# A hybrid mLSTM and sparse-attention block on one core: the first head's products placed later, and the relative-bias rows from split products over the full array

## The chip, the core and the metric
The kernel runs on one core of one Trainium2 chip. The core has a matrix engine (TensorE; PE in the profile, with its weight loads listed as PEld), a vector engine (DVE), a scalar engine (ACT), GpSimd (POOL), a synchronisation engine (SP) that here only issues DMAs, and 16 DMA engines. Every engine works through its own list of instructions in order; an instruction that waits for a semaphore holds up everything behind it on that engine. The metric is the device time of one execution in microseconds.

## The reference, cut to what matters
The block normalises x, multiplies it by one wide input matrix and splits the result into a chunked mLSTM branch (4 heads) and a sparse-attention branch (8 heads); both are gated, mixed and projected, and a gated feed-forward layer follows. Two pieces matter here. In the mLSTM, each head of 1024 positions is cut into 8 chunks of 128:

```python
log_d = jnp.where(causal, bc[..., :, None] - bc[..., None, :] + ic[..., None, :], -jnp.inf)
m_i = jnp.maximum(jnp.max(log_d, axis=-1), log_inter)
P = jnp.exp(log_d - m_i[..., None]) * jnp.einsum('bhcid,bhcjd->bhcij', qc, kc)
num = (jnp.einsum('bhcij,bhcjv->bhciv', P, vc)
       + s_inter[..., None] * jnp.einsum('bhcid,bhcdv->bhciv', qc, C_prev))
```

In the attention, a table of 32 buckets by 8 heads gives a bias for each distance between query and key, the same along every diagonal:

```python
table = rel_bias.astype(jnp.float32).T.reshape(G, R, REL_BUCKETS)
lw = einsum(qb, k_wb) + table[:, :, rel_bucket(dist)]
```

## The kernel before, in words
Stage A normalises and transposes x into two parts whose sum is x (UTH and UTL, in the format that TensorE reads in one pass) and makes the mLSTM values. Stage B, where the change lies, does two things side by side. `b_dense` makes 16 tiles of 128 output columns (q, k and o of each head, and four for the attention). Each tile is two halves of 512 positions; a half is 8 steps, and a step is three products (L277 to L279), called dense products below. `b_aux` makes the gates, then the four mLSTM heads one after the other (`core`), and between them, one at a time from a list called `spare`, the rows of the relative bias (`rel_rows`).

The order is fixed when the program is built. `driver` writes the instructions of both streams into one list: each number that `b_aux` yields is an amount of dense work to be written before it goes on (a dense step counts 648). So a yield moves everything after it, on every engine.

For each dense tile, ScalarE rounds the raw weights into `whi` (L248) and GpSimd makes the rest `wlo` in four instructions (L254): this is the weight split of the tile that comes next. When a half of a q or k tile is done, ScalarE moves it out of PSUM (`padq`, `padk`, L523) and VectorE runs the four-tap convolution on it, one L528 and three L530. Once k is complete, ScalarE loads another function table, applies silu to q and k (L532, L533) and loads the first table again.

A head of the mLSTM: two tables of 128x1024, MB and SB, come from DRAM through SP. GpSimd turns MB into the mask (L682), causal minus MB. `st_a(c)` makes the chunk's product `pa` on TensorE, `E` on ScalarE from the mask (L695), and `PT` and `KW` on VectorE (L698, L699). `st_b(c)` multiplies them with the values into `pn` (L704) and updates the state `CN`; ScalarE copies `pn` to `nd` and squares it (`jk`). A yield of 5000 stands ahead of the first head's `st_a(0)`.

`rel_rows` has four rounds of 480 columns. SP loads a one-hot piece `OH` of 33 rows (L652), TensorE multiplies it with `relt`, 33 rows by 8 heads in plain float32 (L654), VectorE copies the 8 rows out (`rrow`, L656) and GpSimd stores them (`d_row`, L657). Afterwards GpSimd spreads each head's row over 128 rows of DRAM (`d_rep`, L660), which the attention reads much later.

The later stages (gates, attention, output projection and feed-forward by fast matrix multiplication) are not touched by the change.

Of the kernel before, what the change touches and what calls it, by code (L numbers as in the profile page):

```python
# [8 lines left out]
F32 = mybir.dt.float32  # L9
F32R = mybir.dt.float32r  # L10
AF = mybir.ActivationFunctionType
ALU = mybir.AluOpType
PSUM = bass.MemoryType.PSUM

P = 128
T = 1024
NT = 8
# [4 lines left out]
NH = 8  # L22
# [20 lines left out]
def cast32(ap):  # L43
    return ap.bitcast(F32)
# [114 lines left out]
def body(ctx, tc, a, out, stop=None, dbg=None):  # L159
    nc = tc.nc  # L160
# [12 lines left out]
    causal = cst[:, 1, :]  # L173
# [98 lines left out]
    def split_evict(hi, lo, src):  # L272
        nc.scalar.activation(hi, src, AF.Copy)
        nc.vector.tensor_tensor(lo, src, cast32(hi), ALU.subtract)
# [74 lines left out]
    with ExitStack() as sa:  # L349
# [139 lines left out]
        bp = pb_.enter_context(tc.tile_pool(name="stB", bufs=1, reuse_waits="tile"))  # L489
# [75 lines left out]
            for nm, j in order_b1:  # L565
                yield from b_tile(nm, j)

        relt = bp.tile([33, NH], F32, name="relt")
        nc.vector.memset(relt, 1.0)
        nc.scalar.dma_start(relt[0:32, :], a["rel_bias"])  # L570

        def gates():

# [72 lines left out]

        def rel_rows():

            for s in range(4):
                sl = slice(480 * s, 480 * s + 480)  # L650
                OH = bp.tile([33, 480], F32, name=f"OH{s}", tag="OH", bufs=2)
                nc.sync.dma_start(OH, a["oh"][:, sl])  # L652
                pb = psB.tile([P, 512], F32, name=f"pb{s}", tag="Y", bufs=1)
                nc.tensor.matmul(pb[0:NH, 0:480], relt, OH, start=True, stop=True)  # L654
                rrow = bp.tile([NH, 480], F32, name=f"rrow{s}", tag="rrow", bufs=2)
                nc.vector.tensor_copy(rrow, pb[0:NH, 0:480])  # L656
                nc.gpsimd.dma_start(d_row[:, sl], rrow)  # L657
                yield 2600.0
            for h in range(NH):
                nc.gpsimd.dma_start(d_rep[h], d_row[h, :].partition_broadcast(P))  # L660
                yield 650.0

        MBS = {}
        spare = []

        def core_load(h):
            MB = bp.tile([P, NT, P], F32, name=f"MB{h}", tag="MB", bufs=2)
            SB = bp.tile([P, NT, P], F32, name=f"SB{h}", tag="SB", bufs=2)
            for d_, s_ in ((d_M, MB), (d_S, SB)):
                r0 = d_[h:h + 1, :]  # L670
                nc.sync.dma_start(s_, bass.AP(tensor=r0.tensor, offset=r0.offset, ap=[[0, P], [4 * P, NT], [1, P]]))
            MBS[h] = MB, SB

        def core(h, other):

            MB, SB = MBS[h]
# [2 lines left out]
            q3 = qT[h].rearrange("p (c t) -> p c t", c=NT)  # L679
            k3 = kT[h].rearrange("p (c t) -> p c t", c=NT)  # L680
            dec = bp.tile([P, NT], F32, name=f"dec{h}", tag="dec", bufs=2)
            nc.gpsimd.tensor_tensor(MB, causal[:, None, :].to_broadcast([P, NT, P]), MB, ALU.subtract)  # L682
            nc.vector.tensor_copy(dec, SB[:, :, 127])
            nc.vector.tensor_tensor(SB, q3, SB, ALU.mult)
            nd = bp.tile([P, NT, MD + 1], F32, name=f"nd{h}", tag="nd", bufs=2)
# [31 lines left out]
                j_ = bp.tile([P, P], mybir.dt.bfloat16, name=f"jk{h}{c}", tag="jk", bufs=2)  # L717
                nc.scalar.activation(j_, nd[:, c, 0:MD], AF.Square, accum_out=ss[:, 0, c:c + 1])

            yield 5000.0 if h == 0 else 3000.0  # L720
            for c in range(2):
                st_a(c)
                yield 1300.0
# [58 lines left out]
        def b_aux():  # L782
            rel = rel_rows()
            other = []
            spare.extend([lambda: next(rel)] * 12)
            yield from gates()
            core_load(0)
            for h in range(MH):
                if h + 1 < MH:
                    core_load(h + 1)  # L790
                yield from core(h, other)
            while spare:
                spare.pop(0)()
            while other:
                if not other[0][0]():
                    yield None
                else:
                    other.pop(0)[1]()
                    yield 2600.0

        driver(b_dense(), b_aux())
        pb_.close()
        for h in range(4):
# [44 lines left out]
    with ExitStack() as sb:  # L848
        bp = sb.enter_context(tc.tile_pool(name="stB2", bufs=1, reuse_waits="tile"))
# [93 lines left out]
    with ExitStack() as sc:  # L943
# [323 lines left out]
        while any(queues.values()):  # L1267
# [20 lines left out]
            _, op, st = cand  # L1288
# [408 lines left out]
    pb = {}  # L1697
# [242 lines left out]
```

## Time and profile before

| what | value |
|---|---|
| time, median of 3 runs (range) | 1605.21 us (1604.78 to 1607.33) |
| profiled execution: its own time / its span | 1604.37 us / 1602.6 us |
| TensorE busy in the span | 1558.8 us, 97% |
| VectorE / ScalarE / GpSimd busy | 1046.7 (65%) / 742.3 (46%) / 230.7 us (14%) |
| granted TensorE clock, mean | 0.992 of full speed |

The page lists busy time by engine, the span in 40 slices, the chain of work that ended last, and the costliest groups of instructions. Beside it the trace answers questions: who waited for whom, the instructions of an engine in order of time, and the busy times and granted clock in chosen stretches. Stage B lies at about 97 to 320 us of the span; the first head's mask and the four rounds of `rel_rows` lie at 129 to 165 us. Where TensorE is busy nearly all the time, each microsecond in which it waits, or in which its clock is lower, is read in that stretch.

### The profile page before, as it was taken

How to read it: one execution, taken by the hardware profiler on the slowest of the kernel's cores; microseconds unless marked ns; L12 is line 12 of the kernel's file. 1: busy time of each engine (PE TensorE's matmuls, PEld its weight loads, DVE VectorE, ACT ScalarE, POOL GpSimd, SP SyncE). 2: the span in 40 equal slices, each digit the busy share in tenths (PEclk: the TensorE clock that was granted, in tenths of full speed). 3: DMA queues.
4: the chain of work that ended last, by engine and by line, in shares of the span. 5: the costliest groups of instructions: out<-in, count | busy, mean ns of one | idle time of the engine just before them, and what ended most of it. 6: DMA issues, size and time to landing. Idle time of an engine off the chain costs nothing.

```text
span 1602.6 us, 21999 instructions
## 1 busy us (share of the span) xinstructions
PE 1558.8 (97%) x7858; PEld 1317.6 (82%) x7858; DVE 1046.7 (65%) x2214; ACT 742.3 (46%) x1560; POOL 230.7 (14%) x355
## 2 busy tenths in 40 slices
PE   6999999989999999999999989999999999999997
PEld 6876888878989888878887878888888888888876
DVE  6446553235989688840454498666676666978996
ACT  5215455324888688842344244333333333454442
POOL 4013434420113111013000022000000000000130
PEclk9999999999999999999999999999999999999999
DMA  8004532792236422163447212222322223750202
GB/s 254 3 25 100 152 117 97 243 230 86 67 93 103 115 68 85 47 230 106 144 145 269 73 67 92 80 91 80 120 91 79 79 85 113 276 189 22 105 1 105
DMA packets 147358, 181.44 MB, mean 113 GB/s; under 512 B 10414, under 2 KB 105040, under 8 KB 147248
## 3 DMA queue, kind: packets, MB, share of 16 engines
q1 hardware_dynamic: 137440, 157.31, 31.4%
q0 software_dynamic: 9472, 22.06, 5.5%
q8 instruction: 62, 1.02, 0.3%
q10 hardware_dynamic: 336, 0.66, 0.1%
q14 instruction: 48, 0.39, 0.1%
HBM read 137.95 MB, written 49.90 MB: 117 GB/s over the span
## 4 chain that ended last, share of the span: by engine, by line
PE 85%; DVE 3%; DMA 2%; ACT 1%; issue 0%; POOL 0%; SPq 0%; DVEq 0%; ACTq 0%
PE PS L278 15%; PE PS L279 15%; PE PS L277 15%; PE d L277 7%; PE d L279 7%; PE d L278 7%; PE T L1059 4%; PE obank L1081 2%; PE obank L1079 2%; PE br L278 1%; PE br L277 1%; PE br L279 1%; DMA d_ql<-lnq 1%; PE pn L704 1%; DMA raw<-in_w_out 0%; PE pa L692 0%
## 5 line engine op out<-in xcount | busy, mean ns | idle before, releaser
L277 PE MATMUL d<-UTH,whi 128*128 128x512 f32 x576 | 234.4, 407 | 1.8 <-ACT mg L938 0.7
L279 PE MATMUL d<-UTH,wlo 128*128 128x512 f32 x576 | 226.1, 392 | 0.0
L278 PE MATMUL d<-UTL,whi 128*128 128x512 f32 x576 | 225.4, 391 | 0.0
L1441 DVE TENSOR_TENSOR sl<-PS,sl 128x512 f32<-128x512 f32 x182 | 123.8, 687 | 94.9 <-PE PS L279 92.2
L254 POOL TENSOR_TENSOR wlo<-raw,whi 128x256 fp32r<-128x256 f32 x124 | 96.6, 808 | 323.7 <-ACT whi L248 289.9
L279 PEld LDWEIGHTS d<-UTH,wlo 128*128 128x128 f32 x576 | 108.6, 188 | 24.0
L277 PEld LDWEIGHTS d<-UTH,whi 128*128 128x128 f32 x576 | 109.2, 190 | 20.6 <-ACT mg L938 2.0
L278 PEld LDWEIGHTS d<-UTL,whi 128*128 128x128 f32 x576 | 109.3, 190 | 17.2
L1068 DVE TENSOR_TENSOR TL<-T,TH 128x512 fp32r<-128x512 f32 (+1 forms) x184 | 103.3, 581 | 28.8 <-ACT TH L1064 27.9
L1064 ACT ACTIVATE TH<-T 128x512 fp32r<-128x512 f32 (+1 forms) x184 | 90.2, 510 | 26.5 <-PE T L1059 23.6
L1441 DVE TENSOR_TENSOR sl<-sl,sl 128x512 f32<-128x512 f32 (+1 forms) x113 | 77.3, 690 | 17.8 <-ACT sl L1444 12.5
L1444 ACT ACTIVATE sl<-sl 128x512 f32<-128x512 f32 (+1 forms) x85 | 53.4, 631 | 72.0 <-PE PS L278 47.1
L1441 POOL TENSOR_TENSOR acc<-acc 128x512 f32<-128x512 f32 x6 | 9.2, 1546 | 503.5 <-DVE acc L1441 503.4
L1444 ACT ACTIVATE wh<-sl 128x512 fp32r<-128x512 f32 x61 | 38.5, 630 | 81.2 <-PE PS L278 70.0
L1079 PE MATMUL obank<-TH,VHL 128*128 128x256 f32 x264 | 75.6, 310 | 0.0
L1081 PE MATMUL obank<-TL,VHL 128*128 128x256 f32 x264 | 68.4, 283 | 0.4 <-DVE TL L1068 0.4
L277 PE MATMUL PS<-q 128*128 128x512 f32 x172 | 66.9, 389 | 0.0
L278 PE MATMUL PS<-q 128*128 128x512 f32 x172 | 66.9, 389 | 0.0
L279 PE MATMUL PS<-q 128*128 128x512 f32 x172 | 66.9, 389 | 0.0
L1403 DVE TENSOR_TENSOR q<-br,q 128x512 f32<-128x512 f32 x32 | 21.9, 688 | 67.4 <-ACT q L1396 47.4
L1444 ACT ACTIVATE q<-sl 128x512 fp32r<-128x512 f32 x74 | 43.5, 624 | 46.5 <-PE PS L278 29.1
L1441 DVE TENSOR_TENSOR q<-sl,q 128x512 fp32r<-128x512 f32 x72 | 50.2, 734 | 2.8 <-ACT q L1444 2.7
(1289 smaller groups left out, 4256.2 us busy)
## 6 DMA issues: line engine op xcount, KB each, us to landing
raw<-in_w_in SPq DMA_DIRECT2D x40, 512.0 KB, 4.6
ra<-in_w_gate SPq DMA_DIRECT2D x22, 512.0 KB, 5.2
d_gu<-sl SPq DMA_DIRECT2D x44, 256.0 KB, 2.1
q<-d_mg SPq DMA_DIRECT2D x32, 256.0 KB, 3.0
d_rep<-d_row POOLq DMA_DIRECT2D x8, 960.0 KB, 10.3
sl<-d_gu SPq DMA_DIRECT2D x15, 512.0 KB, 5.1
sl<-in_w_down SPq DMA_DIRECT2D x15, 512.0 KB, 5.5
ra<-in_w_up SPq DMA_DIRECT2D x11, 512.0 KB, 3.5
```

Of the source, the lines that this page charges most:

```text
L254: nc.gpsimd.tensor_tensor(lo[:, zs], v[:, zs], cast32(hi)[:, zs], ALU.subtract)
L277: nc.tensor.matmul(ps, ah, bh, start=first, stop=False)
L278: nc.tensor.matmul(ps, ah, bl, start=False, stop=False)
L279: nc.tensor.matmul(ps, al, bh, start=False, stop=last)
L1059: nc.tensor.transpose(pt[:, z, P * r:P * r + P], e, ident)
L1064: nc.scalar.activation(hl[0][:, 0:m], pt[:, 0:m], AF.Copy)
L1068: nc.vector.tensor_tensor(hl[1][:, 0:m], pt[:, 0:m], cast32(hl[0])[:, 0:m], ALU.subtract)
L1079: nc.tensor.matmul(po, vv, th[:, z, :], start=(st[1] == 0), stop=False)
L1081: nc.tensor.matmul(po, vv, tl[:, z, :], start=False, stop=(st[1] == st[2]))
L1403: nc.vector.tensor_tensor(sg[b], ps, sg[b], ALU.mult)
L1441: return pl.step(alts, lambda e: ENG[e].tensor_tensor(out_(), x(), y(), alu), reads, writes, **kw)
L1444: return pl.step((("ACT", cost),), lambda e: nc.scalar.activation(out_(), x(), fn), reads, writes, **kw)
```

## The change
Four edits, all in stage B.

1. The first head's mask is taken out of `core` and called right after the loads of its tables are issued (`mask(0)` in `b_aux`); the other heads call it where it was.
2. The yield ahead of the first head's `st_a(0)` grows from 5000 to 7000.
3. `relt` becomes 128 rows by 128 columns, zero outside the 33 by 8, in two parts (`split_evict`: ScalarE makes the high part, VectorE the low one). It is made when the first round starts, not ahead of the stage.
4. `OH` becomes 128 rows: GpSimd clears it and then issues its load itself (before, SP did). Each round is two products of 128x480 in the one-pass format, and `rrow` has one buffer where it had two.

```diff
-        relt = bp.tile([33, NH], F32, name="relt")
-        nc.vector.memset(relt, 1.0)
-        nc.scalar.dma_start(relt[0:32, :], a["rel_bias"])
+        relr = bp.tile([P, P], F32, name="relr")
+        relt = bp.tile([P, 2, P], F32R, name="relt")
+        nc.vector.memset(relr, 0.0)
+        nc.vector.memset(relr[32:33, 0:NH], 1.0)
+        nc.scalar.dma_start(relr[0:32, 0:NH], a["rel_bias"])
...
         def rel_rows():
+            split_evict(relt[:, 0, :], relt[:, 1, :], relr)
             for s in range(4):
                 sl = slice(480 * s, 480 * s + 480)
-                OH = bp.tile([33, 480], F32, name=f"OH{s}", tag="OH", bufs=2)
-                nc.sync.dma_start(OH, a["oh"][:, sl])
+                OH = bp.tile([P, 480], F32R, name=f"OH{s}", tag="OH", bufs=2)
+                nc.gpsimd.memset(cast32(OH), 0.0)
+                nc.gpsimd.dma_start(OH[0:33, :], a["oh"][:, sl])
                 pb = psB.tile([P, 512], F32, name=f"pb{s}", tag="Y", bufs=1)
-                nc.tensor.matmul(pb[0:NH, 0:480], relt, OH, start=True, stop=True)
-                rrow = bp.tile([NH, 480], F32, name=f"rrow{s}", tag="rrow", bufs=2)
+                for z in range(2):
+                    nc.tensor.matmul(pb[:, 0:480], relt[:, z, :], OH, start=(z == 0), stop=(z == 1))
+                rrow = bp.tile([NH, 480], F32, name=f"rrow{s}", tag="rrow", bufs=1)
                 nc.vector.tensor_copy(rrow, pb[0:NH, 0:480])
                 nc.gpsimd.dma_start(d_row[:, sl], rrow)
...
+        def mask(h):
+            MB, _ = MBS[h]
+            nc.gpsimd.tensor_tensor(MB, causal[:, None, :].to_broadcast([P, NT, P]), MB, ALU.subtract)
...
-            nc.gpsimd.tensor_tensor(MB, causal[:, None, :].to_broadcast([P, NT, P]), MB, ALU.subtract)
+            if h > 0:
+                mask(h)
...
-            yield 5000.0 if h == 0 else 3000.0
+            yield 7000.0 if h == 0 else 3000.0
...
             core_load(0)
+            mask(0)
             for h in range(MH):
```

The yield alone moves instructions on every engine, so the built order is shown at three places. The first is VectorE where the first head begins: qT is the convolution of the second head's q (two halves), PT_0 and KW_0 belong to chunk 0 of the first head. Before:

```order
L530 SCALAR_TENSOR_TENSOR qT_1088<-padq_1086,COLS,qT_1088 128x512 x3
L698 TENSOR_TENSOR PT_0_1175<-pa_0_1170,E_0_1173 128x128
L699 TENSOR_SCALAR KW_0_1176<-pa_0_1170,E_0_1173 128x128
L528 TENSOR_SCALAR qT_1088<-padq_1086,COLS 128x512
L530 SCALAR_TENSOR_TENSOR qT_1088<-padq_1086,COLS,qT_1088 128x512 x3
```

The same place now:

```order
L530 SCALAR_TENSOR_TENSOR qT_1090<-padq_1088,COLS,qT_1090 128x512 x3
L528 TENSOR_SCALAR qT_1090<-padq_1088,COLS 128x512
L530 SCALAR_TENSOR_TENSOR qT_1090<-padq_1088,COLS,qT_1090 128x512 x3
L709 TENSOR_TENSOR PT_0_1197<-pa_0_1192,E_0_1195 128x128
L710 TENSOR_SCALAR KW_0_1198<-pa_0_1192,E_0_1195 128x128
```

The second half's convolution has moved from behind PT_0 and KW_0 to ahead of them. On TensorE, nine dense products have moved from behind the first `pn` to ahead of the first `pa`.

The second place is GpSimd from the first head's mask (MB) to the end of the bias rounds; what an instruction waits for stands in brackets (a name is a semaphore: an engine's, or a DMA's). Before:

```order
L254 TENSOR_TENSOR wlo_1116<-raw_998,whi_1115 128x256 x3
L682 TENSOR_TENSOR MB_1125<-cst,MB_1125 128x1024 [waits DMAHW5_49]
...
L254 TENSOR_TENSOR wlo_1236<-raw_1093,whi_1235 128x256 [waits PE_49,DMAHW3_49,Activation_49,Pool_49]
L657 DMA d_row<-rrow_1260 8x480 [waits DMASW6_49,DVE_49]
...
L657 DMA d_row<-rrow_1384 8x480 [waits DMASW1_49,DVE_49]
L254 TENSOR_TENSOR wlo_1409<-raw_1197,whi_1408 128x256 [waits PE_49,DMAHW1_49,Activation_49,Pool_49]
```

The same place now:

```order
L254 TENSOR_TENSOR wlo_1118<-raw_1000,whi_1117 128x256 x3
L682 TENSOR_TENSOR MB_1127<-cst,MB_1127 128x1024 [waits DMAHW5_49]
...
L254 TENSOR_TENSOR wlo_1223<-raw_1095,whi_1222 128x256 [waits PE_49,DMAHW3_49,Activation_49,Pool_49]
L656 MEMSET OH_1270 128x480
L657 DMA OH_1270<-in_oh 33x480 [waits DMASW6_49,Pool_49]
L663 DMA d_row<-rrow_1276 8x480 [waits DMASW7_49,DVE_49]
L656 MEMSET OH_1309 128x480
...
L663 DMA d_row<-rrow_1366 8x480 [waits DMASW3_49,DVE_49]
L254 TENSOR_TENSOR wlo_1394<-raw_1190,whi_1393 128x256 [waits DMAHW1_49,PE_49,Activation_49]
L656 MEMSET OH_1406 128x480 [waits DMASW0_49]
L657 DMA OH_1406<-in_oh 33x480 [waits DMASW4_49,Pool_49]
L663 DMA d_row<-rrow_1412 8x480 [waits DMASW5_49,DVE_49]
```

The first mask stands behind the same weight split (the the one that ends in `wlo` of the second head's k tile) in both. Each round's one-hot load now stands behind the store of the round before, and the fourth also behind a weight split that came after all four rounds.

The third place is TensorE at the first round: `pb` is its product, `pn` is chunk 1 of the head. Before:

```order
L279 MATMUL d_0_1193<-UTH,wlo_1116 128x512
L654 MATMUL pb_1258<-OH_1256,relt 8x480 [waits DMAHW4_49,DMAHW2_49]
L704 MATMUL pn_1_1263<-MV,PT_1_1204 128x129 [waits DVE_49]
L706 MATMUL pn_1_1263<-CN_1139,SB_1126 128x129 [waits DVE_49]
L709 MATMUL pu_1_1266<-MV,KW_1_1205 128x129
```

The same place now:

```order
L279 MATMUL d_1_1258<-UTH,wlo_1118 128x512
L660 MATMUL pb_1273<-OH_1270,relt 128x480 [waits DMASW6_49,Activation_49,Pool_49]
L660 MATMUL pb_1273<-OH_1270,relt 128x480 [waits DVE_49]
L715 MATMUL pn_1_1279<-MV,PT_1_1215 128x129
L717 MATMUL pn_1_1279<-CN_1141,SB_1128 128x129
```

One instruction has become two; the first waits for the GpSimd-issued load and ScalarE's part of `relt`, the second for VectorE's part. That the round before follows the first half of a dense tile and now follows three steps of the second half comes from the nine products moved above.

## Rows read from the trace of the kernel before
**Rows 1.** Waits of TensorE, whole span: who waited for whom, total us, times, longest.
```profile
PE ph L902 <- DVE lnq L863: 5.7, 1, 5.7
PE pn L704 <- DVE PT L698: 3.3, 1, 3.3
```
**Rows 2.** Timeline of TensorE: start us, us, instruction, count, idle before and its releaser.
```profile
133.66 0.39 PE L278 MATMUL d<-UTL,whi 128*128 128x512 f32 x1
133.89 0.39 PE L279 MATMUL d<-UTH,wlo 128*128 128x512 f32 x1
137.59 0.80 PE L704 MATMUL pn<-MV,PT 128*128 128x129 f32 x2 [3.32 <-DVE PT L698]
...
142.85 0.97 PE L654 MATMUL pb<-OH,relt 33*8 33x480 f32 x2
143.75 0.49 PE L704 MATMUL pn<-MV,PT 128*128 128x129 f32 x2
...
147.71 0.97 PE L654 MATMUL pb<-OH,relt 33*8 33x480 f32 x2
...
157.41 0.97 PE L654 MATMUL pb<-OH,relt 33*8 33x480 f32 x2
```
**Rows 3.** Stretches: length, busy PE, PEld, DVE, ACT, POOL, PEclk, DMA share, GB/s.
```profile
140.00:142.00 2.00, 2.00 (x8) 1.60 (x8) 1.78 (x6) 0.00 (x0) 1.93 (x3) 0.79 0.00 0
360.00:365.00 5.00, 3.80 (x13) 3.44 (x14) 2.29 (x4) 0.00 (x0) 0.55 (x2) 0.50 1.06 301
365.00:370.00 5.00, 5.00 (x27) 4.24 (x27) 0.21 (x1) 0.69 (x1) 0.00 (x0) 0.89 0.11 31
850.00:855.00 5.00, 3.30 (x15) 2.41 (x13) 4.14 (x6) 3.11 (x5) 0.00 (x0) 1.00 0.80 263
```
**Rows 4.** Timeline of VectorE, 109 to 147 us.
```profile
109.59 3.48 DVE L530 SCALAR_TENSOR_TENSOR qT<-padq,COLS,qT 128x512 f32<-128x512 f32 x3
...
132.33 5.00 DVE L530 SCALAR_TENSOR_TENSOR qT<-padq,COLS,qT 128x512 f32<-128x512 f32 x3
...
137.82 0.49 DVE L528 TENSOR_SCALAR qT<-padq,COLS 128x512 f32<-128x512 f32 x1
...
140.59 0.28 DVE L698 TENSOR_TENSOR PT<-pa,E 128x128 f32<-128x128 f32 x1
...
146.51 0.64 DVE L656 COPY rrow<-pb 8x480 f32<-8x480 f32 x1
```
**Rows 5.** Timeline of GpSimd, 129 to 165 us.
```profile
129.60 4.43 POOL L254 TENSOR_TENSOR wlo<-raw,whi 128x256 fp32r<-128x256 f32 x4 [10.23 <-ACT whi L248]
134.00 2.78 POOL L682 TENSOR_TENSOR MB<-cst,MB 128x1024 f32<-128x1024 f32 x1
...
147.45 0.52 POOL L657 DMA_DIRECT2D d_row<-rrow  x1 [4.09 <-DVE CN L713]
...
161.33 2.81 POOL L254 TENSOR_TENSOR wlo<-raw,whi 128x256 fp32r<-128x256 f32 x4 [0.19 <-ACT whi L248]
```
**Rows 6.** Timeline of ScalarE, 136 to 161 us.
```profile
136.82 0.40 ACT L695 ACTIVATE E<-MB,GCOL 128x128 f32<-128x128 f32 x1 [6.72 <-POOL padk L519]
...
152.67 0.69 ACT L523 ACTIVATE padk<-d,COLS 128x512 f32<-128x512 f32 x1 [2.45 <-PE d L279]
...
159.40 0.27 ACT L714 ACTIVATE nd<-pn 128x129 f32<-128x129 f32 x1
...
160.15 1.05 ACT L248 ACTIVATE whi<-raw 128x1024 fp32r<-128x1024 f32 x1
```
**Rows 7.** Small DMAs issued by GpSimd, 80 to 300 us: count, KB each, median us to landing.
```profile
d_row<-rrow POOLq DMA_DIRECT2D x4, 15.0 KB, 2.7
...
d_M<-gall POOLq DMA_DIRECT2D x1, 16.0 KB, 1.7
```
**Rows 8.** The same, 0 to 100 us.
```profile
rows<-in_pe_cmp POOLq DMA_DIRECT2D x1, 16.0 KB, 4.0
```
**Rows 9.** Groups of GpSimd instructions: count, busy us, mean ns, idle before.
```profile
L996 POOL MEMSET E8c<- 128x121 f32 x2 | 0.3, 188 | 0.0
```

## The prediction
> **What bounds the kernel now.** I read the waits of TensorE first: of its long waits, one, 3.3 us for the first head's `PT`, lies in the stage that the change touches [rows 1]. The timeline of TensorE then shows what that wait is worth: the last dense product starts at 133.89, one every 0.23 us, and `pn` starts at 137.59 [rows 2]. That list has no other wait from 138 to 320 us, so there a wait that the change adds is paid in full, and so is one it removes. The third view is the granted clock by stretch. After the wait it is at the lower level (1.2 GHz, 0.50 in the rows) and back at 2.4 GHz 0.84 us after 140: the mean of 140 to 142 is 0.79, which is 0.42 of 2 us at 0.50 [rows 3]. So 3.25 us of work ran at half speed, 1.6 us lost. After the longest wait in that list, 5.7 us, work resumes 1.2 us into the stretch from 360 and the lower level lasts until about 366.1: 4.9 us, 2.45 us lost [rows 1, 3]. Gaps that add up to 1.7 us (850 to 855) leave it at 1.00 [rows 3]. I use these three as prices: about 2 us on top of a wait of several us, nothing on top of one below 2 us.
>
> Last come the engines behind that wait. GpSimd splits weights from 129.60 for 4.43 us and makes the mask from 134.00 for 2.78 [rows 5]; ScalarE's `E` follows at 136.82 [rows 6]; VectorE is in its three L530 from 132.33 for 5.00 us [rows 4]. `PT` is held by both, and both end near 137.3.
>
> **Edit 1, the mask.** In the built order it stands behind the same split on GpSimd as before, so it is ready at 136.8 again and gains nothing. The cover is the order itself: no engine is moved past anything by this edit.
>
> **Edit 2, the yield.** Nine dense products now lie ahead of the wait: 9 x 0.23 = 2.1 us [rows 2]. If `PT` came no later, that would be the gain. But VectorE now has the second half's convolution ahead of `PT`. Its input is ready early (ScalarE no longer has `E` ahead of it), so it starts when the first half ends, at 137.3; alone it takes 140.59 - 137.82 = 2.8 us [rows 4]. ScalarE's next split also moves ahead of `nd`: `E` twice, then `whi`, from 136.8 to about 138.5 [rows 6], and GpSimd's next split begins there, beside the last two of the three L530. Three of them beside a split took 3.48 us where they take 2.3 alone [rows 4], so I add 0.7: `PT` starts at 140.8 and `pn` at 141.1, against 137.59. Net: 141.1 - 137.6 - 2.1 = **+1.4 us**. Bounds: 0.7 (no meeting with GpSimd) to 2.7 (each held up as in the 5.00 us of rows 4). The wait grows from 3.5 to about 5 us, so the clock may cost up to 0.8 more; I leave that in the range.
>
> The row first: the last of the three L530 from 132.33 cannot end until the mask does, since the three end at 137.33 and the mask at 136.78 [rows 4, 5]. The Trainium skill (SBUF — State Buffer, "SBUF: two separate sides") says that a GpSimd instruction that reads SBUF and a VectorE one with two SBUF inputs exclude each other for the whole instruction. The trace agrees; by that rule the split that now meets the convolution blocks it piece by piece, and the sum stays at the 1.4 above.
>
> **Edits 3 and 4 on TensorE.** A plain float32 round takes 143.75 - 142.85 = 0.90 us [rows 2]; two products of 480 columns take 2 x 0.23 x 480/512 = 0.43. Four rounds: **-1.9 us**. The rest of these edits is a matter of what TensorE now waits for.
>
> *Round 1.* The second product needs VectorE's part of `relt`, which stands behind the convolution of `padk`, whose half ends nine dense products earlier. From there: ScalarE 0.69 [rows 6], convolution 2.8, the low part 0.28 as the equal-sized `PT` [rows 4], some 0.3 of hand-overs: 4.1 us. TensorE gets there after 9 x 0.23 + 0.2 = 2.3, or 2.5 with a few products still at the lower clock. Wait **1.6** (0.9 to 1.9).
>
> *Rounds 2 and 3.* Each load is behind the store of the round before. From the second product: its end 0.4, `rrow` 0.64 [rows 4], a hand-over of 0.3 and the store's issue of 0.52 [rows 5], the clearing, then issue to landing. The clearing is not in the trace; 128x121 took 0.19 us [rows 9], four times as wide is 0.5 (at least 0.2, at most 0.75 in proportion). The landing of this load is not there either: small DMAs issued by GpSimd took 1.7, 2.7 and 4.0 [rows 7, 8]; I take 2.7, from the same stretch, and keep both ends. Sum 5.15. TensorE meanwhile has a round of 147.71 - 143.75 = 4.0 us [rows 2] plus 0.1. Waits **1.1 and 1.05** (0.1 to 2.4 each).
>
> The Trainium skill (DMA: Bandwidth & Descriptors, "Anatomy of one DMA — SWDGE (gpsimd) path") puts one such DMA at about 2.0 us plus its bytes over 436 GB/s. For 62 KB that would be an estimate of 2.15; by it the whole sum would be about 1 us lower. No row of the trace has this load from this queue.
>
> *Round 4.* Its load is behind a weight split, and that split waits for ScalarE, which has silu and two table loads ahead of it. Count from where `padk`'s second half starts on ScalarE (152.67 in the rows). To the second `nd` group at 159.40 it is 6.73 us; in the changed order `whi` stands in that place (one group fewer ahead of it than at 160.15), and takes 1.05 [rows 6]. Then the split 2.81 [rows 5], the clearing 0.5, two hand-overs of 0.1, the landing 2.7: 14.0 us. TensorE, from the same point: nine dense products 2.1, the wait of round 3, its products and the transition 0.5, a round 4.0: 6.5 plus 1.05. Wait **6.5** (5.2 with a landing of 1.7; up to 9 with 4.0 and a split slowed to the 4.43 of rows 5). After it the clock is at the lower level as after 360 [rows 3]: **+2.0** (1.6 to 2.45).
>
> *Elsewhere.* The clearing of `relr` and the loads no longer on SP lie beside a busy TensorE: nothing. The second head's mask now stands behind a split and a store; from the end of its tile I count 13.4 us on that path (5.1 on ScalarE, the split, mask, `E` and `PT` of rows 4 to 6, about 2 of `whi`, a store's issue and hand-overs) against 13.4 on TensorE. I put **+0.3** (0 to 1.5).
>
> **Sum.** 1.4 - 1.9 + 1.6 + 1.1 + 1.05 + 6.5 + 2.0 + 0.3 = +12.05 us on the profiled execution's 1604.37 (its span of 1602.6 plus 1.8 around it): 1616.4. The median of the runs is 0.84 higher, so 1617.3, rounded to 1617.
>
> **The rivals.**
>
> *Round 4 is not held by the split* (chance 0.13). If `whi` came early enough, round 4 would wait like rounds 2 and 3, 1.0 instead of 6.5, and the clock would hold: 12.05 - 5.5 - 2.0 = +4.6, 1610. For it: ScalarE's chain up to the split is read from one execution, and part of it is a wait for VectorE. Against: the list puts the split ahead of the clearing, and 6.73 us of ScalarE ahead of the split.
>
> *Slow landings* (0.12). With 4.0 us for each load, rounds 2 and 3 wait 2.4 each and round 4 about 7.7 (round 3's longer wait covers some of it); waits of 2.4 may drop the clock once more (2.0), and the second head waits 1.5. That is 12.05 + 1.3 + 1.35 + 1.2 + 2.0 + 1.2 = +19.1, 1624. For it: 4.0 was seen when weights were loading, and weight loads fall in these rounds. Against: 2.7 is the median here.
>
> *Faster than before* (0.05). `PT` comes no later than 137.6 and the one-hot pieces land while TensorE still has dense work. Then the wait of 3.5 shrinks to 1.4, the clock does not fall (1.6 saved), and the products save 1.9: -2.1 - 1.6 - 1.9 = -5.6, 1600. It decides from the point where the convolution ahead of `PT` would end by 139.7 and the fourth load land by the time TensorE arrives. Against: 2.8 us of convolution that starts at 137.3, and round 4.
>
> *No change* (0.03): waits of some 2 us in all balance the 1.9 saved and the nine products; nothing in the rows points there.
>
> **How the numbers follow.** The forecast has 0.67. From the bounds its own range is 1612 to 1621; with the two slower rivals at 1610 and 1624 the range for 8 in 10 is 1609 to 1624. A measurement of this kernel can tell about 0.2%, 3.2 us, from no change. Faster than 1602.0: 0.05. Within: the 0.03 and a little of the first rival, 0.05. Slower than 1608.4: 0.90.
>
> **What would show it.** In the changed kernel's timeline of TensorE: `pn` of the first head about 5 us after the last dense product, held by `PT`; the second product of round 1 held by VectorE about 1.6 us; rounds 2 and 3 held by the load about 1 us; round 4 held 5 to 9 us, with GpSimd's split and `whi` ending just before, and the granted clock at 0.50 after it. Each round itself should take 0.4 instead of 0.9. I am wrong if round 4 has no wait over 3 us, if `pn` starts before 139.7, or if waits of the same size appear or vanish in a later stage, which I take to be shifted as a whole.

## The result and the profile after

| | before | after |
|---|---|---|
| time, median of 5 runs (range) | 1605.40 us (1604.78 to 1607.33) | 1617.79 us (1616.03 to 1619.72) |
| ratio of the two, 95% interval | | 1.0073 (1.0062 to 1.0085): slower |
| span of the profiled execution | 1602.6 us | 1614.2 us |
| forecast | | 1617 us, 1609 to 1624 |

TensorE's waits in the whole span come first, as who waited for whom, total, times and longest. They answer to [rows 1]:

```profile
PE pb L660 <- DMA OH<-in_oh: 7.9, 3, 6.1
PE ph L914 <- DMA w<-in_w_cmp: 6.8, 1, 6.8
PE pn L715 <- DVE PT L709: 5.0, 1, 5.0
...
PE pb L660 <- DVE relt L274: 1.1, 1, 1.1
...
PE pn L717 <- DVE CN L724: 0.6, 1, 0.6
```

The wait for `PT` grew from 3.3 to 5.0 us, and the rounds, which had no wait, now have four. TensorE's timeline shows where; it answers to [rows 2]:

```profile
135.66 0.39 PE L279 MATMUL d<-UTH,wlo 128*128 128x512 f32 x1
141.05 0.80 PE L715 MATMUL pn<-MV,PT 128*128 128x129 f32 x2 [5.00 <-DVE PT L709]
...
146.61 0.46 PE L660 MATMUL pb<-OH,relt 128*128 128x480 f32 x1
148.13 0.48 PE L660 MATMUL pb<-OH,relt 128*128 128x480 f32 x1 [1.07 <-DVE relt L274]
...
153.10 0.67 PE L660 MATMUL pb<-OH,relt 128*128 128x480 f32 x2 [0.75 <-DMA OH<-in_oh]
153.61 0.38 PE L715 MATMUL pn<-MV,PT 128*128 128x129 f32 x2
...
158.59 0.68 PE L660 MATMUL pb<-OH,relt 128*128 128x480 f32 x2 [1.07 <-DMA OH<-in_oh]
...
169.10 1.14 PE L660 MATMUL pb<-OH,relt 128*128 128x480 f32 x2 [6.09 <-DMA OH<-in_oh]
170.04 0.63 PE L715 MATMUL pn<-MV,PT 128*128 128x129 f32 x2
```

A round without a wait inside it now takes 153.61 - 153.10 = 0.51 us where it took 0.90. VectorE's timeline shows what held `pn` and the second product of round 1; it answers to [rows 4]:

```profile
132.06 5.08 DVE L530 SCALAR_TENSOR_TENSOR qT<-padq,COLS,qT 128x512 f32<-128x512 f32 x3
137.06 0.47 DVE L528 TENSOR_SCALAR qT<-padq,COLS 128x512 f32<-128x512 f32 x1
137.57 3.23 DVE L530 SCALAR_TENSOR_TENSOR qT<-padq,COLS,qT 128x512 f32<-128x512 f32 x3
140.72 0.28 DVE L709 TENSOR_TENSOR PT<-pa,E 128x128 f32<-128x128 f32 x1
...
145.55 2.33 DVE L530 SCALAR_TENSOR_TENSOR kT<-padk,COLS,kT 128x512 f32<-128x512 f32 x3
147.79 0.28 DVE L274 TENSOR_TENSOR relt<-relr,relt 128x128 fp32r<-128x128 f32 x1
```

Twice three L530, with an L528 between them, stand without a stop in front of `PT`, the second three beside the split from 138.39. GpSimd's timeline, which answers to [rows 5], shows round 4:

```profile
138.39 3.67 POOL L254 TENSOR_TENSOR wlo<-raw,whi 128x256 fp32r<-128x256 f32 x4 [1.77 <-issue]
...
149.59 0.52 POOL L663 DMA_DIRECT2D d_row<-rrow  x1 [6.26 <-DVE rrow L662]
150.10 0.52 POOL L656 MEMSET OH<- 128x480 f32 x1
150.91 0.52 POOL L657 DMA_DIRECT2D OH<-in_oh  x1 [0.29 <-POOL OH L656]
...
163.38 2.77 POOL L254 TENSOR_TENSOR wlo<-raw,whi 128x256 fp32r<-128x256 f32 x4 [2.62 <-ACT whi L248]
166.09 0.50 POOL L656 MEMSET OH<- 128x480 f32 x1
166.88 0.55 POOL L657 DMA_DIRECT2D OH<-in_oh  x1 [0.29 <-POOL OH L656]
```

The last one-hot piece is issued at 166.88 behind a split that waited for `whi`, while TensorE has stood still since 163.0. ScalarE's timeline has that `whi` 6.74 us behind `padk`, where the prediction worked out 6.73 from [rows 6]:

```profile
155.51 0.69 ACT L523 ACTIVATE padk<-d,COLS 128x512 f32<-128x512 f32 x1 [0.40 <-PE d L279]
...
162.25 1.05 ACT L248 ACTIVATE whi<-raw 128x1024 fp32r<-128x1024 f32 x1
```

The last view is the granted clock by stretch (the columns of [rows 3]):

```profile
141.00:143.00 2.00, 1.95 (x8) 1.95 (x9) 1.00 (x4) 0.57 (x2) 1.70 (x4) 0.50 0.00 0
143.00:145.00 2.00, 2.00 (x6) 1.53 (x6) 0.55 (x2) 0.76 (x2) 0.33 (x1) 0.55 0.76 209
145.00:147.00 2.00, 1.99 (x9) 1.16 (x7) 1.90 (x3) 0.12 (x1) 0.00 (x0) 1.00 0.30 85
...
169.00:171.00 2.00, 1.90 (x7) 1.79 (x8) 0.65 (x1) 0.00 (x0) 0.00 (x0) 0.50 0.04 8
171.00:173.00 2.00, 2.00 (x11) 1.82 (x11) 0.90 (x3) 0.92 (x5) 0.51 (x1) 0.72 0.05 8
```

After the waits of 5.0 and 6.1 us the clock is at the lower level (0.50), and back at 1.00 some 3 to 4 us later. The waits of 0.75 to 1.07 have no such stretch behind them: 150 to 163 stands at 1.00.

**Where the 11.6 us of span arise.** The same product can be found in both timelines, and the difference of its two start times is what has been lost up to there. The nine dense products moved ahead (2.07 us) have to be taken off it.

| product | before | after | lost, less 2.07 | what came in |
|---|---|---|---|---|
| `pn`, chunk 0 | 137.59 | 141.05 | 1.39 | first head |
| `pn`, chunk 1 | 143.75 | 148.46 | 2.64 | round 1, clock 0.24 |
| `pn`, chunk 2 | 148.61 | 153.61 | 2.93 | round 2 |
| `pn`, chunk 3 | 153.46 | 159.11 | 3.58 | round 3 |
| `pn`, chunk 4 | 158.31 | 170.04 | 9.66 | round 4 |
| second dense product behind it, L278 | 159.64 | 172.28 | 10.57 | clock after it, 0.91 |

At 310 us of before, the end of stage B, where the nine products are made up, 11.6 us are lost: 1.0 more, of which 0.2 came with the second head and 0.8 in the third, where TensorE waits 0.58 us for `CN`. Behind it the difference wanders between 11.2 and 12.7 and ends at 11.6.

### The profile page after: what moved, and what is told of

It is laid out like the page before. It is cut to its first block, busy times and chain, and to the rows that moved or that the text cites. A ratio compares the mean times of both kernels' runs of the same rounds, so it can differ in the third digit from the quotient of the medians.

```text
span 1614.2 us, 22013 instructions
## 1 busy us (share of the span) xinstructions
PE 1556.6 (96%) x7858; PEld 1317.9 (82%) x7858; DVE 1053.5 (65%) x2216; ACT 743.1 (46%) x1561; POOL 235.4 (15%) x363
## 4 chain that ended last, share of the span: by engine, by line
PE 88%; DVE 4%; DMA 4%; issue 2%; POOL 1%; ACT 1%; DVEq 0%; SPq 0%; POOLq 0%; ACTq 0%
PE PS L277 15%; PE PS L278 15%; PE PS L279 15%; PE d L277 7%; PE d L279 7%; PE d L278 7%; PE T L1071 4%; PE obank L1093 2%; PE obank L1091 2%; PE br L279 2%; PE br L277 2%; PE br L278 2%; DMA d_ql<-lnq 1%; PE mv L277 1%; PE mv L279 1%
## 5 line engine op out<-in xcount | busy, mean ns | idle before, releaser
L278 PE MATMUL d<-UTL,whi 128*128 128x512 f32 x576 | 225.4, 391 | 0.0
L278 PEld LDWEIGHTS d<-UTL,whi 128*128 128x128 f32 x576 | 109.1, 189 | 16.9
L278 PE MATMUL PS<-q 128*128 128x512 f32 x172 | 66.9, 389 | 0.0
```

The lines of the kernel that those rows point to most:

```text
L278: nc.tensor.matmul(ps, ah, bl, start=False, stop=False)
```

## The experiments

All were timed in alternation with the kernel before. Names: "7000" and "5000" are the first head's yield.

**1. The yield alone.** Edits 1 and 2 in the kernel before; the rows as they were.

```diff
-            yield 5000.0 if h == 0 else 3000.0
+            yield 7000.0 if h == 0 else 3000.0
```

> The kernel before with edits 1 and 2 alone (the mask call and the yield of 7000); the bias rows as before. Theory A (each wait comes from the place that an instruction got in its engine's list): VectorE has the second half's convolution ahead of PT, as in the changed kernel, so pn starts at about 141 after a wait of 5.0 us, and the net of it is what the changed kernel showed there: 141.05 - 137.59 = 3.46, less nine products of 0.23, plus 0.24 of clock: +1.6 us, 1607.0. No wait at the four rounds: the weight split that moves ahead of the fourth store holds nobody on TensorE. Rival B (the later start disturbs more than the first head): the rounds and the second head shift against the weight splits and TensorE waits there too, 3 us or more in all.

Measured: 1610.53 against 1605.59 us, ratio 1.0029 (1.0018 to 1.0041). More than A's 1.6, and not by B's mechanism either: no round waits. TensorE's timeline has two waits in stage B:

```profile
141.56 0.80 PE L709 MATMUL pn<-MV,PT 128*128 128x129 f32 x2 [5.66 <-DVE PT L703]
...
232.12 0.49 PE L711 MATMUL pn<-CN,SB 128*128 128x129 f32 x2 [0.58 <-DVE CN L718]
```

`pn` is 0.5 later than in the changed kernel, mostly because the second three L530 took 3.56 us beside their split, not 3.23; the lower clock behind it lasted until 146.9, not 144.8, and cost 1.0 us more than before, not 0.24. At the end of stage B 3.9 us are lost, 0.9 of them in the third head. The rest of the 6.4 us between the two spans came behind it, in stages that no edit touches (TensorE's wait at `ph` is 6.6 us here, 5.7 before, and one for `q` near 856 us is 3.0, 1.8 before). It is one execution each, so whether that belongs to the kernel stays open.

**2. The rows alone.** The changed kernel with the yield at 5000.

> The changed kernel with the yield at 5000: the bias rows by split products, but no products moved. In the built order the fourth one-hot load is then ahead of the weight split. Theory A: round 4 waits like rounds 2 and 3, about 1 us, and the 6 us are gone with the clock that follows; round 1 is worse, since its load stands behind a split that ends at 143.4 (3.3 us from 140.07) and TensorE is there at 142.85: 143.4 + 0.8 of clearing + 2.2 to land = 146.4, and the low part of relt comes behind a convolution that ends at about 146.5: 4 us in all, with about 1 us of clock. Sum: 4 + 1 + 3 x 0.9 - 4 x 0.39 = +6.1 us, 1611.5. Rival B (the edits add up): all that the changed kernel lost less the 1.6 of the yield, 11.6 - 1.6 = +10, 1615.4, with round 4 still waiting about 6 us.

Measured: 1616.21 us, ratio 1.0065 (1.0052 to 1.0077). The time is near B's, the mechanism is neither's. TensorE's timeline:

```profile
148.55 0.92 PE L660 MATMUL pb<-OH,relt 128*128 128x480 f32 x2 [4.66 <-DMA OH<-in_oh]
...
159.59 0.68 PE L660 MATMUL pb<-OH,relt 128*128 128x480 f32 x2 [0.81 <-DMA OH<-in_oh]
...
166.66 0.68 PE L660 MATMUL pb<-OH,relt 128*128 128x480 f32 x2 [2.65 <-DMA OH<-in_oh]
```

Round 4 waits 2.65 us, not 6.1: with the split behind its load the large wait is gone, as A has it. What is left above 1 us is VectorE's, whose timeline has round 3's copy behind a convolution, so that the store and the load behind it are late:

```profile
160.06 2.33 DVE L530 SCALAR_TENSOR_TENSOR kT<-padk,COLS,kT 128x512 f32<-128x512 f32 x3
162.30 0.64 DVE L662 COPY rrow<-pb 8x480 f32<-8x480 f32 x1
```

Round 1 waits 4.66 us: its load is issued at 144.85, behind a split, and takes 3.6 us to land. The two parts of the change are therefore not a sum. Alone they cost 4.9 and 10.6 us (differences of medians), together 12.4 (against the before of its own runs); at the end of stage B 3.9, 8.8 and 11.6 are lost. With the yield at 7000 round 1 does not wait for its load, for two reasons of about the same size: TensorE comes 2.7 us later (146.61; here it stands from 143.89), and the load is issued 2.1 us earlier (142.79), since the split ahead of it also moved. The same move puts round 4 behind the next split.

**3. The one-hot pieces early.** The changed kernel, with the four pieces cleared and loaded ahead of the gates.

```diff
+        for s in range(4):
+            ...
+            nc.gpsimd.memset(cast32(OH), 0.0)
+            nc.gpsimd.dma_start(OH[0:33, :], a["oh"][:, 480 * s:480 * s + 480])
+            OHS.append(OH)
```

> The changed kernel with all four one-hot pieces cleared and loaded ahead of the gates, in two tiles that the mLSTM's outputs use later; all else the same. Theory A: the waits for the loads go, 0.75 + 1.07 + 6.09 = 7.9 us, and with the last one the 1.3 us at the lower clock behind it: 9.2 us less than the changed kernel, 1608.6; round 1 keeps its 1.1 us for the low part of relt, pn of the first head its 5.0. Rival B (the wait is turned into another): the store, the weight split or the second head's mask holds TensorE next, and less than half of the 9.2 us comes back: 1613 or more.

Measured: 1609.28 us, ratio 1.0017 (1.0008 to 1.0025), 8.5 us below the changed kernel. In stage B TensorE keeps three waits: `PT` 5.68, `relt` 1.12 and `CN` 0.58. Theory A: the loads held the rounds, and nothing took their place; the 0.7 us short of A's 9.2 match the longer wait for `PT`.

**4. And relt early.** Its two parts are made at the stage's start too.

```diff
+        split_evict(relt[:, 0, :], relt[:, 1, :], relr)
         OHS = []
```

> As the run with the early one-hot pieces, and the two parts of relt are made there too. Theory A: round 1's 1.07 us go as well: 1607.5, no wait at any round, and the rest over the kernel before is the first head (+1.6), the later heads (about +1.7 between 180 and 310 us) less the four rounds (4 x 0.39 = 1.6). Rival B (round 1 waits for its load or its bank, not for relt): no change from the run with early pieces, 1608.6.

Measured: 1607.89 us, ratio 1.0018 (1.0009 to 1.0027). Between the two theories' times the interval can't tell; the trace can. Round 1 waits no more, but TensorE's timeline has a new wait:

```profile
99.79 0.39 PE L601 MATMUL pg<-cst,gif 128*32 128x128 f32 x2 [1.45 <-DVE gif L597]
...
141.75 0.80 PE L722 MATMUL pn<-MV,PT 128*128 128x129 f32 x2 [3.96 <-DVE PT L716]
```

VectorE's low part of `relt` now stands ahead of the gates' first copy, a wait that neither theory named. In this execution it cost little in the end: TensorE reaches the first head later and waits 3.96 us for `PT` instead of 5.68, and `pn` starts at 141.75, with the early pieces alone at 141.64. Whether the 1.1 us of round 1 came back in the time stays open, as the medians are 1.4 us apart and the intervals nearly the same.

**5. The same with 5000.**

> Split products with one-hot pieces and both parts of relt made ahead of the gates (as in the run early_both), and the yield back at 5000. Theory A (the yield costs through the convolution that it puts ahead of PT, and through the later heads): the first head is as before, a wait of 3.3 to 3.7 us with the clock behind it, no wait at the rounds, four rounds 0.39 us shorter: 1605.5 - 1.6 = 1603.9. Rival B (making the rows from split products costs something else that is still there, as early_both's 2.3 us over before might mean): 1606 to 1608, no better than the run with the yield at 7000.

Measured: 1606.07 us, ratio 1.0003 (0.9994 to 1.0011): no change. By its time this is B, something else is still there, and the trace names it: the wait at `pg`, 1.57 us, which A's figure lacked; with it A gives 1605.5. Nothing covers it at 5000, where `pn` starts at 139.76, 2.2 us later than before. No round waits, so the split products gain what the wait takes.

**6. The mask really first.** Experiment 5's kernel, with the tables' loads and the mask inside the gates, one yield earlier.

```diff
             yield 2600.0
+            core_load(0)
+            mask(0)
             pq = psB.tile([P, 512], F32, name="pq", tag="Y", bufs=1)
...
-            core_load(0)
-            mask(0)
             for h in range(MH):
```

> As rows_ready_y5000, but the first head's tables are loaded and its mask made one step of the gates earlier, so that in the built order GpSimd has the mask ahead of the weight split, and the yield is 5600: three more dense products ahead of pn, the second half's convolution still behind PT. Theory A: MB lands at about 126.1 and the mask runs from there to 128.6, ahead of the split. The third of the three L530 no longer runs beside the mask: PT at about 135.2 where it was 137.25, pn at 135.5, dense products until 134.8, a wait of 0.7 us and no fall of the clock. 137.6 + 0.7 - 135.5 = 2.8, the clock 1.6, the rounds 1.6: 6.0 less than before, 1599.5. Rival B (the convolution is slow beside any GpSimd work and ends when the split does, near 137): the wait stays above 2 us and the gain is that of rows_ready_y5000 and the three products, about 1603.

> As mask_first_y5600 with the yield at 7000, so that VectorE has the second half's convolution ahead of PT again. Theory A: the first half's convolution ends at 135.1, the second runs beside the next weight split (3.3 instead of 2.3 us, and 0.5 for L528) to 138.9, pn at 139.3, where dense products end at 136.1: a wait of 3.2 us and the lower clock behind it. Against before 139.3 - 137.6 - 2.1 = -0.4, rounds -1.6, later heads +1.2: 1604.7, some 5 us worse than with 5600. Rival B (it was the late mask that held PT, not the convolution): the wait is gone at 7000 too, and it is within 1 us of the run with 5600.

> As mask_first_y5600 with the yield at 5000: the mask's part by itself. Theory A: PT at 135.2 again, dense products only until 134.1, a wait of 1.4 us, which is below the 1.7 us that left the clock at its upper level: 0.7 us more than with 5600, 1600.2. Rival B: as 1603 in the run with 5600, or the wait of 1.4 us is long enough for the clock to fall, 1.6 us more.

Measured: with 5600 1605.31 us (ratio 1.0000, 0.9991 to 1.0008), with 7000 1606.24 (1.0006, 0.9997 to 1.0015), with 5000 1603.06 (0.9985, 0.9976 to 0.9994). A was wrong on which yield is best, and too low by 1.5 to 6 us; all three still have the wait of 1.45 us at `pg`, which A leaves out. At `pn` the three waited 1.71, 3.59 and 0.98 us. That 7000 is the worst there, though the mask was done early, is A's point: it is the convolution that holds `PT`. GpSimd's timeline with 7000 has

```profile
128.51 2.43 POOL L691 TENSOR_TENSOR MB<-cst,MB 128x1024 f32<-128x1024 f32 x1 [7.00 <-DMA MB<-d_M]
```

VectorE's has the second half's convolution until `PT`

```profile
138.72 3.00 DVE L530 SCALAR_TENSOR_TENSOR qT<-padq,COLS,qT 128x512 f32<-128x512 f32 x3
141.65 0.28 DVE L718 TENSOR_TENSOR PT<-pa,E 128x128 f32<-128x128 f32 x1
```

and TensorE's

```profile
141.98 0.49 PE L724 MATMUL pn<-MV,PT 128*128 128x129 f32 x2 [3.59 <-DVE PT L718]
```

But with 5600 four more waits came in the later heads, 1.10, 0.55, 1.10 and 0.38 us between 178 and 258, and none over 0.2 with 5000.

**7. The mask alone.** The kernel before with experiment 6's move and nothing else.

> The kernel before with one thing changed: the first head's tables are loaded and its mask made one step of the gates earlier, ahead of the weight split. Rows of the bias and the yield as before. Theory A (the mask's place is worth what mask_first_y5000 showed at pn, and the split products are worth 0.39 us a round): a wait of about 1 us for PT in place of 3.3, no fall of the clock: -1.3 (the net of mask_first_y5000 up to pn) - 1.5 (it carried 1.0 to 1.4 us of late gates into pn) - 1.5 (clock): about -3.5 us at 143, 1602.0. Rival B (the gain was the rows'): within 1 us of before.

Measured: 1601.72 against 1604.80 us, ratio 0.9976 (0.9967 to 0.9986): theory A. GpSimd's timeline has the mask ahead of the split:

```profile
125.99 2.39 POOL L678 TENSOR_TENSOR MB<-cst,MB 128x1024 f32<-128x1024 f32 x1 [6.94 <-DMA MB<-d_M]
129.28 4.99 POOL L254 TENSOR_TENSOR wlo<-raw,whi 128x256 fp32r<-128x256 f32 x4 [0.90 <-DVE dec L690]
```

and TensorE's has at `pn`

```profile
135.07 0.49 PE L711 MATMUL pn<-MV,PT 128*128 128x129 f32 x2 [1.01 <-DVE PT L705]
```

The mask starts when its table lands, and `pn` starts 2.5 us earlier than in [rows 2], at the upper clock (130 to 145 stands at 1.00). The tables' loads moved with the mask, but their place gained nothing: the first is issued at 119.65 here and at 119.97 before, where the whole stage runs 0.3 us later.

**8. Both, with relt after the gates' columns, and the later heads' masks.** The second kernel has 5600, and makes each later mask during the head before.

```diff
             nc.vector.tensor_scalar(ECOL, pq[:, 32:64], float(MD ** 0.5), None, ALU.mult)
+            split_evict(relt[:, 0, :], relt[:, 1, :], relr)
```

> As mask_first_y5000, but the two parts of relt are made after the gates' last columns, not at the stage's start, where VectorE's part stood ahead of the gates' first copy and TensorE waited 1.45 us for it. Theory A: that wait goes and nothing takes its place: 1603.1 - 1.5 = 1601.6, and 1.5 us less than mask_alone_y5000 would be if nothing else differs. Rival B (the start of the gates has slack behind it, since PT is bound by the tables' landing): no gain, 1603.

> As best_y5000 with the yield at 5600 and the masks of the later heads made during the head before (after its chunk 5), so that they stand ahead of the weight split again. Theory A (the 2 to 3 us that 5600 lost were the second head's mask behind a split: waits of 1.10, 0.55, 1.10 and 0.38 us between 178 and 258): these waits go, and three products more cover the first head's wait: 1601.6 - 0.7 = 1600.9. Rival B (the waits come from VectorE's order, not from the mask): they stay, 1603 or more.

Measured: with 5000 1600.57 against 1604.80 us, ratio 0.9971 (0.9959 to 0.9982), the fastest here and about what A says (4.2 us below before, A's 1601.6 is 3.9 below the before of experiment 6); with 5600 1604.43 (0.9994, 0.9985 to 1.0003). In the first the wait at `pg` is gone and the four rounds take 0.4 us less each, but it is only 1.2 us below the mask alone, and the two intervals overlap. TensorE's timeline shows part of why it is not more: with one buffer for `pb`, round 2 waits for round 1's copy, which stands behind a convolution on VectorE.

```profile
135.22 0.49 PE L724 MATMUL pn<-MV,PT 128*128 128x129 f32 x2 [0.63 <-DVE PT L718]
143.91 0.71 PE L669 MATMUL pb<-OH,relt 128*128 128x480 f32 x2 [0.66 <-DVE rrow L671]
```

With 5600 the second head's wait for `PT` went with the mask's move, but those for `CN` grew (0.55 and 1.10 us in experiment 6; 0.51, 1.14 and 1.32 here): theory B for the larger part. Why VectorE's order is worse there was not taken apart.

## Why the prediction was right, by its steps

The time (1617 against 1617.79) and every named place of stage B up to round 4 came out; the sizes, in us:

| step | forecast | measured |
|---|---|---|
| first head, net | +1.4 | +1.4, clock 0.2 more |
| four rounds of products | -1.9 | -1.3 (0.1 in round 1, 0.39 in the others) |
| round 1, `relt` | 1.6 | 1.07 |
| rounds 2 and 3, load | 1.1, 1.05 | 0.75, 1.07 |
| round 4, load behind the split | 6.5 | 6.09 |
| clock after round 4 | 2.0 | 1.3 (0.42 in the round, 0.91 behind it) |
| second head | +0.3 | +0.2 |
| third head | no term | +0.8 |

**First head.** The convolution ahead of `PT` is shown as the cause: with the mask ready at 131 us, the kernel with 7000 still waits 3.59 us (experiment 6). That the net came out at the forecast 1.4 is in part luck. The changed kernel is 0.25 us ahead when stage B begins (its first dense product starts at 96.07, before at 96.32), so that the first head itself lost about 1.6. And with the same order on VectorE other executions waited 5.66 and 5.68 us, or 3.96 where TensorE came late (experiment 4): the meeting with the split cost 0.9 to 1.2 in three of them and 0.4 in the last, the working has 0.7.

**Edit 1** gained nothing, by the cover that was named: the split stays ahead of the mask. Experiment 7 shows what a mask that does come earlier is worth, 3 us.

**Rounds 2 to 4.** The mechanism is shown twice: with the loads early the three waits go and 8.5 us come back, and with the split behind the fourth load its wait falls from 6.1 to 2.65. The landing was mis-sized. Of the four loads in the changed kernel the view of the tile `OH` says:

```profile
DMA to landing us min/median/max: 2.1/2.2/3.7
```

2.2 us, not 2.7. By that alone rounds 2 and 3 would have waited 0.5 to 0.6; the 0.29 us between the clearing and the load, which the working of these rounds does not have, and, in round 3, a slower issue (0.77 us) and landing (2.4) took part of it back in round 2 and all of it in round 3, whose 1.05 is thus met by errors that cancel. The Trainium skill (DMA: Bandwidth & Descriptors, "Anatomy of one DMA — SWDGE (gpsimd) path") gave an estimate of 2.15; the trace agrees for three of the four loads (2.1 to 2.4). The 3.7 is the first load, beside a weight load (159 GB/s moved while it was under way, 25 to 30 beside the others). So the rival with slow landings had a true price, but in a round where TensorE came later anyway.

**Missing: the third head.** "Elsewhere" puts +0.3 on the second head and nothing on the third, which lost 0.8: it waits for `CN` in every run with 7000, in none with 5000. VectorE's timeline of the changed kernel shows why:

```profile
238.15 0.71 DVE L753 SCALAR_TENSOR_TENSOR ss<-nd 128x8 f32<-128x8 f32 x1
238.89 0.65 DVE L754 TENSOR_TENSOR ss<-ss,ECOL 128x8 f32<-128x8 f32 x1
239.47 0.34 DVE L724 SCALAR_TENSOR_TENSOR CN<-CN,dec,pu 128x129 f32<-128x129 f32 x1
```

The update of `CN` stands behind two small operations on the squares, `ss`, which the order with 7000 puts behind a convolution; before, they stood ahead of it (222.55) and took 0.16 and 0.17 us. Here they run beside a split that starts at 237.74. The stages behind B were shifted as a whole, within 1.1 us.

**The sum** is within 0.5 us of the profiled execution (+12.05 forecast, +11.6 measured; +12.4 by the medians) in part by luck: rounds 1, 2 and 4 and the clock behind them came out 2.0 below their terms, the products, the first head's clock and the later heads 1.5 above. Three of its own additions are also off: the pieces named for rounds 2 and 3 make 5.06, not 5.15, TensorE's side of round 4 makes 6.6, not 6.5, and the second head's path makes 13.9 before its hand-overs, not 13.4. The sum was treated as additive, and for this kernel it held; experiments 1 and 2 show that the terms are tied to each other by the order, since each half alone costs other waits than it does beside the other half.

## What to carry to other kernels

A load issued on a compute engine's queue costs what that queue has ahead of it, not its own time: here 0.5 us of issue and 2.2 of landing became a wait of 6.1 us. Before an operation is called earlier in the program, look where it lands in its engine's list, since a call that moved past nothing gave nothing and the same call one yield earlier gave 3 us. A yield that covers one wait moves every other engine's list too, so the two halves of a change have to be timed apart and together.

## What the runs showed of the hardware

GpSimd and VectorE held each other up, here for a whole instruction. VectorE's timeline of the run with the yield at 5600 and the later masks moved has, beside a mask that ran from 125.83 to 128.25,

```profile
125.87 2.53 DVE L274 TENSOR_TENSOR relt<-relr,relt 128x128 fp32r<-128x128 f32 x1 [2.55 <-ACT relt L273]
```

an instruction that takes 0.28 us alone. In experiment 8's run with 5000 it started together with the mask, not 0.04 us behind it, and was not held up; VectorE's timeline there has

```profile
126.15 0.29 DVE L274 TENSOR_TENSOR relt<-relr,relt 128x128 fp32r<-128x128 f32 x1 [2.55 <-ACT relt L273]
```

In experiment 4 an L528, which reads one tile and a column of factors, began at 136.06 beside a mask that ended at 138.42:

```profile
136.06 2.68 DVE L528 TENSOR_SCALAR qT<-padq,COLS 128x512 f32<-128x512 f32 x1
```

It takes 0.48 alone. Three L530 beside a split of four pieces took 2.7 to 3.6 us instead of 2.33, and the split, 2.77 us while VectorE stood idle (163.38 in the changed kernel), took up to 4.99 beside VectorE's work (129.28 in experiment 7).

Waits of up to 2.65 us (round 4 of experiment 2) left TensorE at the upper level in these runs; those from 3.3 to 6.1 us in stage B were each followed by 2.9 to 5.3 us at the lower one, in experiment 6 with 7000 from 1 us after the work had begun again. Clearing 128x480 took 0.50 us on GpSimd, as estimated from the 128x121 of [rows 9].
